# Convolution output weights cast by halves ahead of the norm, and later transposes behind the attention, in a two-layer fp32 decoder trunk

## The chip, the cores and the metric

The kernel runs on one core of one Trainium2 chip. The metric is the device time of one execution in microseconds (us); before the change the median of three runs is 2128.0 us (2128.0 to 2129.94).

## The reference, cut to what matters

There is one sequence of T = 1024 tokens with D = 1024 features. Layer 0 mixes tokens with a causal conformer convolution, layer 1 with sliding-window attention. Each layer adds the mixer's result to the stream and normalises, does the same around a squared-ReLU MLP, and adds a gated embedding.

```python
def conformer_conv(x, w_in, b_in, w_dw, b_dw, ln_g, ln_b, w_out, b_out):
    h = x @ w_in + b_in
    a, gate = jnp.split(h, 2, axis=-1)
    h = a * jax.nn.sigmoid(gate)
    h = lax.conv_general_dilated(h, w_dw[:, None, :], ...) + b_dw
    h = jax.nn.silu(layer_norm(h, ln_g, ln_b))
    return h @ w_out + b_out

def reference(x, p, ...):
    for i in range(DEPTH):                       # DEPTH = 2
        y = conformer_conv(...) if i < 1 else swa_sink_attention(...)
        x = layer_norm(DEEPNORM_ALPHA * x + y, mix_ln_g[i], mix_ln_b[i])
        x = layer_norm(DEEPNORM_ALPHA * x + sq_relu_mlp(x, ...), mlp_ln_g[i], mlp_ln_b[i])
        x = x + (p[i] @ ple_w_proj[i]) * jax.nn.sigmoid(x @ ple_w_gate[i])
    return x
```

## The kernel before

Every fp32 product is three matmuls on split operands. `split` casts a source to a high part (`wh` for weights, `xTh` for the transposed stream) on ScalarE, and VectorE subtracts to get the low part (`wl`, `xTl`); `mm3` then issues high by high, high by low and low by high. The stream is held as 8 tiles of 128 tokens, each in two halves of 512 features, and, transposed, as `xTh` and `xTl` in 8 blocks `kb` of 128 features.

Weights come as units of 128 x 1024, which are two blocks `kb` of 512 output columns. `prep` (L542) loads a unit into one of two `raw` buffers, casts it (L558) and subtracts (L559) into one of five `wh` and `wl` buffers. A `raw` buffer takes its next load only when both instructions of the unit before last have read it. The convolution's output projection `w_out` has eight units, here called U0 to U7: U0 to U3 hold the first 512 output columns, U4 to U7 the others. `mix_out` (L1048) makes them, and it alone gives `prep` a `gate`, an instruction that the load may not be ordered before. `tok_group` then holds four output banks in PSUM (names `ps`), one for each of four token tiles, and goes through the units.

The end of the convolution's norm is a chain over four engines: VectorE and GpSimd scale rows of tiles `X` and `A` by `sm`; TensorE transposes four 128 x 128 blocks into a bank; ScalarE applies SiLU from the bank (`z<-tr,cst` or `z<-ps,cst`); then `xTh` and `xTl` follow. Three banks rotate for the transposes, so every transpose waits for the `z` three before it. In this time ScalarE also copies the last tiles of the embedding product (`t<-ps`), which SyncE stores to `proj`. SyncE then loads eight pieces `E<-in_x_dram` of the stream.

In layer 1 the attention's output projection is finished by `out_tiles`, which calls `layer_norm` (L631) for each token tile. That normalises the tile in place on VectorE (tiles `A` and `B`) and calls `to_xT` (L603), which transposes both halves (`transpose4`) and splits them.

Nothing is issued as it is written. `Recorder.record` collects all instructions. `Recorder.schedule` walks them greedily with estimated costs and picks, on each engine, the ready one with the lowest place `prio`, which is the place of recording plus an offset that `later` sets. `slack` is added to the planned readiness of a marked instruction, so the plan treats its data as that much later; it adds no wait on the chip. The order on each engine is then fixed, and the chip keeps the order and waits by semaphores. Since `issue` emits every instruction from one line, all rows of the profile have the line L480.

Of the kernel before, what the change touches and what calls it, by code (L numbers as in the profile page):

```python
# [10 lines left out]
F32 = mybir.dt.float32  # L11
F32R = mybir.dt.float32r
AF = mybir.ActivationFunctionType
ALU = mybir.AluOpType
# [7 lines left out]
HT = 512  # L22
# [60 lines left out]
        2: [("weight",)], 3: [("out", 0)], 5: [("out", 1)],  # L83
    },
)
CST = 256 + 2 * NH
LANDING = dict(scr=4000.0, qd=5000.0, kd=5000.0, ad=5500.0, zd=6500.0, wsum=5000.0, proj=4500.0, xsp=4000.0, hid=4500.0)
SLACK = 900.0
# [424 lines left out]
class Emit:  # L513
# [28 lines left out]
    def prep(self, ap, blocks=None, gate=None):  # L542

        nc = self.nc
        raw = nc.tile("raw", (P, 1024), F32)
        wh = nc.tile("wh", (P, 1024), F32R)
        wl = nc.tile("wl", (P, 1024), F32R)
        if blocks:
            for j, kb in enumerate(blocks):
                cs = slice(j * 256, (j + 1) * 256)  # L550

                nc.sync.dma_start(raw[:, cs], ap[:, cs])
                self.split(raw[:, cs], wh[:, cs], wl[:, cs])
                self.load_xT(0, kb, nc.sync if kb else nc.scalar)
            return wh, wl
        with nc.after(gate) if gate else contextlib.nullcontext():
            nc.sync.dma_start(raw, ap)
        nc.scalar.copy(wh, raw)  # L558
        nc.vector.tensor_tensor(out=wl, in0=raw, in1=wh.bitcast(F32), op=ALU.subtract)  # L559
        return wh, wl  # L560

    def split(self, src, h, l):
# [37 lines left out]
    def blocks(self, a):  # L600
        return [a[:, j * P : (j + 1) * P] for j in range(4)]

    def to_xT(self, xt, t):  # L603

        for q in range(2):
            pv = self.transpose4(self.blocks(xt[q]), SLACK).rearrange("p (a b) -> p a b", a=4)
            sl = (slice(None), slice(4 * q, 4 * q + 4), slice(t * P, (t + 1) * P))
            self.split(pv, self.xTh[sl], self.xTl[sl])

# [22 lines left out]
    def layer_norm(self, t, gb, spill=None):  # L632

        nc = self.nc
        xt = self.x[t]
        mean, scale = self.stats(xt)
        for q in range(2):
            nc.vector.scalar_tensor_tensor(out=xt[q], in0=xt[q], scalar=mean, in1=gb[0][q], op0=ALU.subtract, op1=ALU.mult)
        for q in range(2):
            nc.vector.scalar_tensor_tensor(out=xt[q], in0=xt[q], scalar=scale, in1=gb[1][q], op0=ALU.mult, op1=ALU.add)  # L640
        self.to_xT(xt, t)
        if spill:
            for q in range(2):
                v = self.sb(("X", "zz")[q])
                nc.scalar.mul(v, xt[q], ALPHA)
                nc.sync.dma_start(spill[t][:, q * HT : (q + 1) * HT], v)
# [21 lines left out]
    def setup(self):  # L668
        nc, d = self.nc, self.d
        self.cc = self.const("cst", (P, CST), F32)[:, 0 : 32 + 64 + CG]  # L670
        self.ident = self.const("ident", (P, P), F32)
# [940 lines left out]
    def attention(self):  # L1612
        nc, d, ws = self.nc, self.d, self.ws
        ac = self.sb("cst", n=CST)
        nc.sync.dma_start(ac[:, 0:256], d["aconst"])
# [343 lines left out]
```

## Time and profile before

| | before |
|---|---|
| median of three runs | 2128.0 us |
| the profiled execution | 2127.52 us |
| its span, first to last instruction | 2125.8 us |
| TensorE (PE) busy | 2115.8 us |
| VectorE (DVE) busy | 1560.1 us |
| ScalarE (ACT) busy | 1046.2 us |
| GpSimd (POOL) busy | 201.1 us |

1.7 us lie around the span of the profiled execution. In timelines the columns are the start of a row, its length, engine, line, operation, output and inputs by their names without numbers, shape, and the count of instructions joined in the row; a bracket tells the idle time before it and what released it. PE and DVE records overlap a little, so the price of an instruction is read from one start to the next.

### The profile page before, as it was taken

Reading aid. Unit: us, or ns where it says so; the run is one execution under the profiler, and the core shown is the slowest. Engines: PE = TensorE matmul, PEld = TensorE weight load, DVE = VectorE, ACT = ScalarE, POOL = GpSimd, SP = SyncE. Lnnn points to the kernel's source line nnn. Section 1 sums busy time; section 2 is a strip of 40 time slices with the busy share of each in tenths; the row PEclk is TensorE's granted clock in tenths of the full one; section 3 lists DMA queues with packets and bytes.
Section 4 is the critical chain, followed back from the end, with each engine's and each line's share of the span. In section 5 each row is a group of like instructions: output and inputs, shape, how many; then the busy total and the mean of one; then the engine's idle time right before and its main releaser. Section 6 shows DMA issues by size and latency. Waiting matters only on the chain.

```text
span 2125.8 us, 28547 instructions
## 1 busy us (share of the span) xinstructions
PE 2115.8 (100%) x10067; PEld 1762.0 (83%) x10067; DVE 1560.1 (73%) x2359; ACT 1046.2 (49%) x1888; POOL 201.1 (9%) x391
## 2 busy tenths in 40 slices
PE   9999999999999999999999999999999999999999
PEld 7888888888888888888889888888888888888887
DVE  8766868966566787889554798796755658878993
ACT  7555743555555433341333797365555563333321
POOL 0000141000000200000000566100000011000010
PEclk9999999999999999999999999999999999999999
DMA  7679882347457955540567672364654598445223
GB/s 249 195 204 278 279 216 99 105 163 258 168 179 277 257 184 172 179 129 25 167 194 224 213 239 63 111 197 146 223 187 136 182 339 238 149 160 189 88 70 104
DMA packets 208078, 384.61 MB, mean 181 GB/s; under 512 B 28736, under 2 KB 82496, under 8 KB 207936
## 3 DMA queue, kind: packets, MB, share of 16 engines
q1 hardware_dynamic: 200880, 369.96, 53.0%
q0 software_dynamic: 6912, 12.59, 3.3%
q8 instruction: 79, 1.29, 0.2%
q14 instruction: 63, 0.52, 0.1%
q10 hardware_dynamic: 144, 0.26, 0.0%
HBM read 263.98 MB, written 114.56 MB: 178 GB/s over the span
## 4 chain that ended last, share of the span: by engine, by line
PE 95%; DVE 2%; DMA 2%; ACT 1%; issue 0%; POOL 0%; SPq 0%; DVEq 0%; ACTq 0%; POOLq 0%
PE ps L480 73%; PE tr L480 22%; DMA raw<-in_w_up_dram 1%; DVE A L480 1%; DVE wl L480 0%; DMA wh<-hid 0%; ACT z L480 0%; DVE sm L480 0%; DMA X<-in_xT_dram 0%; ACT t L480 0%; DVE t L480 0%; ACT wh L480 0%; DVE xTl L480 0%; POOL sm L480 0%; SPq L480 0%
## 5 line engine op out<-in xcount | busy, mean ns | idle before, releaser
L480 DVE TENSOR_TENSOR wl<-raw,wh 128x1024 fp32r<-128x1024 f32 (+2 forms) x144 | 151.6, 1053 | 141.4 <-ACT wh L480 141.1
L480 PE MATMUL ps<-xTl,xTh 128*128 128x512 f32 x628 | 244.3, 389 | 0.0
L480 PE MATMUL ps<-xTh,xTl 128*128 128x512 f32 x628 | 244.3, 389 | 0.0
L480 PE MATMUL ps<-xTh 128*128 128x512 f32 x628 | 244.1, 389 | 0.0
L480 PE MATMUL ps<-xTh,wh 128*128 128x512 f32 x608 | 238.7, 393 | 0.4 <-ACT xTh L480 0.3
L480 PE MATMUL ps<-xTl,wh 128*128 128x512 f32 x608 | 238.6, 392 | 0.1
L480 PE MATMUL ps<-xTh,wl 128*128 128x512 f32 x608 | 237.8, 391 | 0.0
L480 ACT CAST wh<-raw 128x1024 fp32r<-128x1024 f32 (+2 forms) x144 | 131.4, 913 | 200.8 <-PE ps L480 98.4
L480 PE MATMUL ps<-wl,xTh 128*128 128x512 f32 (+1 forms) x424 | 162.3, 383 | 0.0
L480 PE MATMUL ps<-wh,xTh 128*128 128x512 f32 (+1 forms) x424 | 161.5, 384 | 0.0
L480 PE MATMUL ps<-wh,xTl 128*128 128x512 f32 (+1 forms) x424 | 160.8, 380 | 0.4 <-DVE xTl L480 0.4
L480 DVE TENSOR_TENSOR wl<-g,wh 128x512 fp32r<-128x512 f32 x140 | 92.5, 686 | 90.0 <-ACT wh L480 90.0
L480 ACT CAST wh<-g 128x512 fp32r<-128x512 f32 x140 | 82.7, 621 | 150.1 <-PE ps L480 98.3
L480 ACT CAST xTh<-wh 128x1024 fp32r<-128x1024 f32 x78 | 81.9, 1050 | 123.2 <-PE ps L480 101.5
L480 PEld LDWEIGHTS ps<-xTl,xTh 128*128 128x128 f32 x628 | 117.9, 188 | 24.6
L480 PEld LDWEIGHTS ps<-xTh,xTl 128*128 128x128 f32 x628 | 117.9, 188 | 24.4
L480 PEld LDWEIGHTS ps<-xTh 128*128 128x128 f32 x628 | 117.9, 188 | 24.3
L480 PEld LDWEIGHTS ps<-xTh,wh 128*128 128x128 f32 x608 | 114.3, 188 | 25.8 <-ACT xTh L480 1.0
L480 PEld LDWEIGHTS ps<-xTh,wl 128*128 128x128 f32 x608 | 114.2, 188 | 23.4
L480 PEld LDWEIGHTS ps<-xTl,wh 128*128 128x128 f32 x608 | 114.3, 188 | 22.2 <-DVE xTl L480 0.8
L480 DVE TENSOR_TENSOR xTl<-wh,xTh 128x1024 fp32r<-128x1024 f32 x78 | 95.1, 1220 | 32.9 <-ACT xTh L480 32.8
L480 DVE TENSOR_TENSOR xTl<-wl,xTh 128x1024 fp32r<-128x1024 f32 x80 | 97.3, 1218 | 3.4 <-ACT xTh L480 3.4
(318 smaller groups left out, 4952.6 us busy)
## 6 DMA issues: line engine op xcount, KB each, us to landing
wh<-hid SPq DMA_DIRECT2D x80, 512.0 KB, 4.5
raw<-in_w_up_dram SPq DMA_DIRECT2D x64, 512.0 KB, 3.8
wl<-in_w_down_dram SPq DMA_DIRECT2D x60, 512.0 KB, 4.6
hid<-t SPq DMA_DIRECT2D x95, 256.0 KB, 2.4
hid<-zz SPq DMA_DIRECT2D x68, 256.0 KB, 3.5
raw<-hid SPq DMA_DIRECT2D x30, 512.0 KB, 4.3
z<-scr SPq DMA_DIRECT2D x32, 256.0 KB, 3.9
proj<-t SPq DMA_DIRECT2D x32, 256.0 KB, 3.8
```

The costliest lines, as they stand in the source:

```text
L480: getattr(getattr(nc, o.eng), o.name)(*a, **k)
```

## The change

Two things change. `prep` casts gated units, which are the eight of `w_out`, in two halves of 512 columns, and records cast and subtraction 100 places sooner. The load itself keeps its place and gate. `to_xT` takes its slack as an argument, and the norm behind the attention (the one that spills to `self.mid[1]`) gives 1700 where it gave 900; all other norms keep 900.

```diff
+HALVES = slice(0, HT), slice(HT, 2 * HT)
+SEAM = 1700.0
+SOONER = 100
 ...
 def prep(self, ap, blocks=None, gate=None):
         with nc.after(gate) if gate else contextlib.nullcontext():
             nc.sync.dma_start(raw, ap)
-        nc.scalar.copy(wh, raw)
-        nc.vector.tensor_tensor(out=wl, in0=raw, in1=wh.bitcast(F32), op=ALU.subtract)
+        with nc.later(-SOONER if gate else 0):
+            for c in HALVES if gate else (slice(0, 2 * HT),):
+                self.split(raw[:, c], wh[:, c], wl[:, c])
         return wh, wl
 ...
-    def to_xT(self, xt, t):
+    def to_xT(self, xt, t, slack):
         for q in range(2):
-            pv = self.transpose4(self.blocks(xt[q]), SLACK).rearrange("p (a b) -> p a b", a=4)
+            pv = self.transpose4(self.blocks(xt[q]), slack).rearrange("p (a b) -> p a b", a=4)
 ...
 def layer_norm(self, t, gb, spill=None):
-        self.to_xT(xt, t)
+        self.to_xT(xt, t, SEAM if spill is self.mid[1] else SLACK)
```

The order changes on ScalarE at the end of the convolution's norm. Before, the row of whole casts ahead of the first `z` holds U0 (`raw_617`) and U1 (`raw_630`), and U2 (`raw_742`) is cast behind the three copies `t`.

```order
L480 ACTIVATE X_600_2393<-X_600_2393,sm_61_125 128x512
L480 ACTIVATE A_592_2366<-A_592_2366,sm_61_125 128x512
L480 CAST wh_628_2519<-raw_617_2478 128x1024
L480 CAST wh_706_2962<-raw_630_2524 128x1024
L480 ACTIVATE z_688_2860<-tr_713_3014,cst_337 128x512
```

```order
L480 CAST xTh_340<-z_755_3212 128x512
L480 COPY t_718_3049<-ps_717_3040 128x512
L480 ACTIVATE z_760_3238<-tr_758_3222,cst_337 128x512
L480 COPY t_721_3062<-ps_719_3055 128x512
L480 CAST xTh_340<-z_760_3238 128x512
L480 COPY t_723_3073<-ps_720_3058 128x512
L480 CAST wh_739_3154<-raw_742_3171 128x1024
```

Now the same two stretches read as follows.

```order
L483 ACTIVATE X_600_2393<-X_600_2393,sm_61_125 128x512
L483 ACTIVATE A_592_2366<-A_592_2366,sm_61_125 128x512
L483 CAST wh_628_2519<-raw_617_2478 128x512 x2
L483 CAST wh_706_2962<-raw_630_2524 128x512
L483 ACTIVATE z_688_2860<-tr_713_3014,cst_337 128x512
```

```order
L483 CAST xTh_340<-z_754_3211 128x512
L483 CAST wh_706_2962<-raw_630_2524 128x512
L483 COPY t_718_3049<-ps_717_3040 128x512
L483 CAST wh_739_3154<-raw_742_3176 128x512
L483 ACTIVATE z_764_3256<-tr_757_3223,cst_337 128x512
L483 CAST wh_739_3154<-raw_742_3176 128x512
L483 CAST xTh_340<-z_764_3256 128x512
L483 ACTIVATE z_767_3274<-ps_758_3236,cst_337 128x512
L483 COPY t_721_3062<-ps_719_3055 128x512
L483 COPY t_723_3073<-ps_720_3058 128x512
```

Three halves instead of two whole casts stand ahead of the first `z`; U1's second half and both halves of U2 stand ahead of the last two copies `t`, and one `z` has passed the copies.

On SyncE's queue, at the loads for `w_out`, two units (U2 and U3) stood ahead of the `proj` stores before.

```order
L480 DMA raw_742_3171<-in_w_out_dram 128x1024
L480 DMA raw_749_3188<-in_w_out_dram 128x1024
L480 DMA proj_5_88_152<-t_718_3049 128x512
L480 DMA proj_6_89_153<-t_721_3062 128x512
L480 DMA proj_7_90_154<-t_723_3073 128x512
L480 DMA E_702_2946<-in_x_dram 128x512 x2
L480 DMA E_710_2983<-in_x_dram 128x512 x2
L480 DMA E_712_3009<-in_x_dram 128x512 x2
L480 DMA E_714_3027<-in_x_dram 128x512 x2
```

Now U3 (`raw_790`) stands behind the stores and the eight loads of the stream.

```order
L483 DMA raw_742_3176<-in_w_out_dram 128x1024
L483 DMA proj_5_88_152<-t_718_3049 128x512
L483 DMA proj_6_89_153<-t_721_3062 128x512
L483 DMA proj_7_90_154<-t_723_3073 128x512
L483 DMA E_702_2946<-in_x_dram 128x512 x2
L483 DMA E_710_2983<-in_x_dram 128x512 x2
L483 DMA E_712_3009<-in_x_dram 128x512 x2
L483 DMA E_714_3027<-in_x_dram 128x512 x2
L483 DMA raw_790_3378<-in_w_out_dram 128x1024
L483 DMA raw_801_3415<-in_w_out_dram 128x1024
```

U3's load has moved behind eleven transfers, and U4's (`raw_801`) follows it directly; the other rows kept their places.

On TensorE, behind the attention, the last token tiles have four transposes of tiles `A` (the rows with `ident`), here called T1 to T4. Before, they stood so among the matmuls of the next product:

```order
L480 MATMUL ps_2330_13119<-ident_338,A_2245_12629 128x128 x4
L480 MATMUL ps_2346_13194<-wh_2318_13063,wh_2328_13109 128x512
L480 MATMUL ps_2340_13167<-ident_338,A_2250_12657 128x128 x4
L480 MATMUL ps_2346_13194<-wl_2317_13061,wh_2328_13109 128x512
L480 MATMUL ps_2346_13194<-wh_2318_13063,wl_2326_13104 128x512
```

```order
L480 MATMUL ps_2347_13198<-wl_2317_13061,wh_2328_13109 128x512
L480 MATMUL ps_2343_13174<-ident_338,A_2252_12665 128x128 x4
L480 MATMUL ps_2347_13198<-wh_2318_13063,wl_2326_13104 128x512
L480 MATMUL tr_2352_13217<-wh_2318_13063,wh_2269_12742 128x512
L480 MATMUL tr_2352_13217<-wl_2317_13061,wh_2269_12742 128x512
L480 MATMUL tr_2352_13217<-wh_2318_13063,wl_2268_12740 128x512
L480 MATMUL tr_2352_13217<-wh_2318_13063,wh_2328_13109 128x512
L480 MATMUL tr_2352_13217<-wl_2317_13061,wh_2328_13109 128x512
L480 MATMUL ps_2369_13281<-ident_338,A_2253_12667 128x128 x4
L480 MATMUL tr_2352_13217<-wh_2318_13063,wl_2326_13104 128x512
```

Now the last two and their neighbours read:

```order
L483 MATMUL tr_2352_13233<-wh_2318_13079,wh_2269_12758 128x512
L483 MATMUL tr_2352_13233<-wl_2317_13077,wh_2269_12758 128x512
L483 MATMUL tr_2352_13233<-wh_2318_13079,wl_2268_12756 128x512
L483 MATMUL ps_2343_13190<-ident_338,A_2252_12681 128x128 x4
L483 MATMUL ps_2373_13307<-ident_338,A_2253_12683 128x128 x4
L483 MATMUL tr_2352_13233<-wh_2318_13079,wh_2325_13109 128x512
L483 MATMUL tr_2352_13233<-wl_2317_13077,wh_2325_13109 128x512
```

T1 and T2 stand three matmuls later, T3 four; T4 stands two matmuls sooner, directly behind T3.

## The prediction

> **What bounds the kernel now.** The head of the page comes first: the span, the busy time of the engines and the chain of work that ended last.
>
> ```profile
> span 2125.8 us, 28547 instructions
> PE 2115.8 (100%) x10067; PEld 1762.0 (83%) x10067; DVE 1560.1 (73%) x2359; ACT 1046.2 (49%) x1888; POOL 201.1 (9%) x391
> PE 95%; DVE 2%; DMA 2%; ACT 1%; issue 0%; POOL 0%; SPq 0%; DVEq 0%; ACTq 0%; POOLq 0%
> ```
>
> TensorE is the bound: 2125.8 - 2115.8 = 10 us of the span are not its work. The change neither adds nor removes TensorE work, so it can gain only from that rest. The table of waits says which part.
>
> ```profile
> PE ps L480 <- DVE t L480: 1.5, 1, 1.5
> PE ps L480 <- ACT t L480: 1.2, 2, 0.7
> PE ps L480 <- DVE A L480: 0.7, 2, 0.5
> PE tr L480 <- ACT z L480: 0.7, 1, 0.7
> PE ps L480 <- DVE xTl L480: 0.4, 1, 0.4
> ```
>
> The change's two places own three rows: `z` and `xTl` at the end of the convolution's norm (0.7 + 0.4 us) and `A` behind the attention (0.7 us in two waits). If all went and nothing came, that would be 1.8 us, 0.09%. About 0.2% (4.3 us) is what a measurement of this kernel can tell from no change, so a measurable gain is as good as excluded. The question is what new wait could arise.
>
> The TensorE timeline at the first place:
>
> ```profile
> 264.47 0.40 PE L480 MATMUL ps<-wh,wl 128*128 128x512 f32 x1
> 265.60 0.66 PE L480 MATMUL tr<-ident,X 128*128 128x128 f32 x4 [0.73 <-ACT z L480]
> ...
> 268.35 0.50 PE L480 MATMUL ps<-wh,xTl 128*128 128x512 f32 x1 [0.37 <-DVE xTl L480]
> ...
> 283.46 1.30 PE L480 MATMUL ps<-wh,xTh 128*128 128x512 f32 x5
> 284.60 0.39 PE L480 MATMUL ps<-wl,xTh 128*128 128x512 f32 x1
> ```
>
> After the two stalls TensorE runs without a gap; five matmuls take 284.60 - 283.46 = 1.14 us, so one takes 0.228.
>
> **Part 1: what the halves save.** ScalarE and VectorE there:
>
> ```profile
> 262.89 1.98 ACT L480 CAST wh<-raw 128x1024 fp32r<-128x1024 f32 x2
> 264.77 0.77 ACT L480 ACTIVATE z<-tr,cst 128x512 f32<-128x512 f32 x1
> 265.44 0.76 ACT L480 ACTIVATE z<-ps,cst 128x512 f32<-128x512 f32 x1
> ...
> 268.47 0.63 ACT L480 CAST xTh<-z 128x512 fp32r<-128x512 f32 x1
> 268.98 0.79 ACT L480 ACTIVATE z<-ps,cst 128x512 f32<-128x512 f32 x1
> ...
> 272.97 0.63 ACT L480 COPY t<-ps 128x512 f32<-128x512 f32 x1
> 273.45 1.11 ACT L480 CAST wh<-raw 128x1024 fp32r<-128x1024 f32 x1
> 274.40 0.83 ACT L480 ACTIVATE z<-ps,cst 128x512 f32<-128x512 f32 x1
> ```
>
> ```profile
> 265.28 1.21 DVE L480 TENSOR_TENSOR wl<-raw,wh 128x1024 fp32r<-128x1024 f32 x1
> 266.41 1.29 DVE L480 TENSOR_SCALAR X<-X,sm 128x512 f32<-128x512 f32 x2
> 267.62 0.67 DVE L480 TENSOR_TENSOR xTl<-z,xTh 128x512 fp32r<-128x512 f32 x1
> ```
>
> From start to start, a whole cast takes 274.40 - 273.45 = 0.95 us, a 512-column cast 268.98 - 268.47 = 0.51, a `z` 265.44 - 264.77 = 0.67, a copy `t` 273.45 - 272.97 = 0.48; on VectorE a whole `wl` 266.41 - 265.28 = 1.13, one 512-column step (267.62 - 266.41) / 2 = 0.605, which I take for half a `wl`. Three half casts instead of two whole ones ahead of the first `z`: 3 x 0.51 - 2 x 0.95 = -0.37 us, so the first stall shrinks by 0.37. Three half subtractions instead of two whole ones: 3 x 0.605 - 2 x 1.13 = -0.44, so `X` and the first `xTl` come 0.44 earlier. TensorE passes both stalls about **0.44 us earlier**; at most the whole 0.73 + 0.37 = 1.10 goes.
>
> Splitting costs 2 x 0.51 - 0.95 = 0.07 us on ScalarE and 2 x 0.605 - 1.13 = 0.08 on VectorE per unit. [...]
>
> **Part 2: what the halves delay.** SyncE's queue:
>
> ```profile
> 265.31 1.54 SPq L480 DMA_DIRECT2D raw<-in_w_out_dram  x2
> 271.47 2.48 SPq L480 DMA_DIRECT2D proj<-t  x3
> 274.04 4.91 SPq L480 DMA_DIRECT2D E<-in_x_dram  x8
> ...
> 284.46 2.67 SPq L480 DMA_DIRECT2D raw<-in_w_out_dram  x2
> ```
>
> Before, U2 and U3 were issued at 265.3. Now U3's `raw` buffer comes free only after U1's second half is cast and subtracted, and its load stands behind three `proj` stores and eight loads of `E`. When do these end? The stores wait for the last copy `t`. ScalarE has no slack that could absorb extra work ahead of it:
>
> ```profile
> 263.00:284.00 21.00, 19.89 (x117) 16.15 (x116) 17.55 (x29) 20.88 (x32) 15.71 (x12) 1.00 0.74 226
> ```
>
> (busy columns are PE, PE load, DVE, ACT, POOL: ACT 20.88 of 21.00.) Ahead of that copy now stand six half casts for two whole ones and one `z` more: 6 x 0.51 - 2 x 0.95 + 0.67 = 1.83 us. So it starts at 274.80, the `E` loads are issued from 275.9 to 280.8 instead of 274.04 to 278.95, and U3's load goes out at about 280.8.
>
> When does it land? The issue table for one late `E` load (issued at 278.5) and one `raw` load (issued at 284.5), each with KB and us to landing, and the window between:
>
> ```profile
> E<-in_x_dram SPq DMA_DIRECT2D x1, 256.0 KB, 9.8
> ```
>
> ```profile
> raw<-in_w_out_dram SPq DMA_DIRECT2D x1, 512.0 KB, 6.9
> ```
>
> ```profile
> 280.00:284.00 4.00, 4.00 (x23) 3.33 (x22) 3.87 (x7) 3.88 (x7) 0.88 (x1) 1.00 1.10 268
> ```
>
> The DMA engines are full (share 1.10, 268 GB/s), so a load lands when what is queued ahead has drained. Before, the late `E` load landed at 278.5 + 9.8 = 288.3; now that is between 288.3 (the queue drains as before) and 290.15 (1.83 later), middle 289.2. U3's 512 KB behind it take 1.95 us at 268 GB/s, or twice that if GpSimd's loads of `B` get half; middle 2.9. Landing: about **292.1**, outer ends 287.7 (280.8 + 6.9) and 294.0.
>
> When is it wanted? Behind the place at 283.46, now 283.02, TensorE has 33 matmuls to U3's first one (24 of U2, 9 of other units): 283.02 + 33 x 0.228 = 290.5. The first half cast adds 0.51 and about 0.1 of signalling: 292.1 + 0.6 - 290.5 = **2.2 us of new stall**; from 287.7 it would be none, from 294.0 it would be 4.1. The matching subtraction (0.605) is covered by the three `wh` matmuls of other banks that now stand first (0.68). U4, directly behind U3, is wanted only after 24 matmuls of U3 and another group; but VectorE must subtract U4 before it empties the first output bank, which may cost up to 0.2 more. Later loads have room. I put nothing for these.
>
> **Part 3: transposes behind the attention.** At the last tiles TensorE and VectorE do this:
>
> ```profile
> 1396.46 0.63 PE L480 MATMUL ps<-ident,A 128*128 128x128 f32 x4 [0.25 <-DVE A L480]
> ...
> 1399.89 0.63 PE L480 MATMUL ps<-ident,A 128*128 128x128 f32 x4 [0.50 <-DVE A L480]
> ...
> 1401.75 0.62 PE L480 MATMUL ps<-ident,A 128*128 128x128 f32 x4
> ```
>
> ```profile
> 1399.66 1.28 DVE L480 TENSOR_TENSOR xTl<-ps,xTh 128x512 fp32r<-128x512 f32 x2
> 1400.86 0.74 DVE L480 SCALAR_TENSOR_TENSOR A<-A,sm,g 128x512 f32<-128x512 f32 x1
> ```
>
> T1, three matmuls later, loses its wait of 0.25, T3, four later (0.9 us), its 0.50. But T4 now follows T3 directly. Its tile needs the step that was at 1400.86, which VectorE now does ahead of the two `xTl`, and its bank is T1's, free only after T1's `xTl`. That comes at about 1399.66 + 0.74 + 0.605 = 1401.0, so T4 starts near 1401.1. Without stalls TensorE would be there at 1401.75 - 0.75 - 2 x 0.228 = 1400.5, so T4 waits about 0.55. Gain: 0.75 - 0.55 = **0.2 us**, between 0 and 0.75. The earlier tiles of this norm are reordered in the same way; none of their transposes has a row among the waits, and later places leave their data more time, so I put nothing for them.
>
> **Sum.** -0.44 + 2.2 - 0.2 = +1.6 us on the profiled execution: 2127.5 + 1.6 = 2129.1 (span 2125.8 + 1.6 = 2127.4; 1.7 around it). The median of before lies 0.5 above that execution, so I forecast a median of **2129.6 us**.
>
> **The rivals.**
>
> *U3 lands in time* (0.25). Speaking for it: 6.9 us to landing for a `raw` load behind the same kind of traffic gives 287.7. Against: a 256 KB load issued earlier took 9.8. Then only gains are left: 2128.0 - 0.44 - 0.2 = 2127.4, at the outside 2126.2 with all 1.8 us.
>
> *U3 lands very late and TensorE falls back to its starting speed* (0.11, the slower side). The first matmuls of the trace:
>
> ```profile
> 1.51 3.35 PE L480 MATMUL ps<-t 128*128 128x512 f32 x7 [1.51 <-DVE t L480]
> ```
>
> Seven take 3.35 us, 0.48 each instead of 0.228. If the stall is long enough to bring that back, a first stretch of 3.35 us loses 3.35 - 7 x 0.228 = 1.75. With U3 at the late end and 0.2 for the output bank: 4.1 + 1.75 + 0.2 - 0.64 = +5.4, hence 2133.4. The total passes 4.3 us when the stall passes 4.3 + 0.64 - 1.75 - 0.2 = 3.0, that is when U3 lands after 292.9. Against it: later waits in this trace are 0.7 us at most, so nothing shows that a stall of 3 brings the slow start back; and the granted clock (the column ahead of the DMA share) reads 1.00 in that stretch too, so it may have another cause:
>
> ```profile
> 1.50:5.00 3.50, 3.35 (x7) 2.15 (x7) 0.38 (x1) 1.83 (x3) 0.00 (x0) 1.00 0.85 250
> ```
>
> [...]
>
> *The head does not gain and the tail does not stall* (0.09). Only U1's first half is ahead of the norm, its `wl` second half comes 12 us later, and T4 pays back T3: 2128.0. For it: every term here is under 2.5 us; against: the second stall's releaser is plainly the subtraction that has been cut.
>
> The forecast has 0.55. Its own ends are 2128.0 - 0.64 = 2127.4 with no stall and 2128.0 + 4.1 + 0.2 - 0.64 = 2131.7 without the clock. The range goes from 2126.5, for the case of gains, to 2132.5; most of the slow case lies beyond. Slower by over 0.2% means over 2132.3: 0.11, the second rival. Faster by over 0.2% needs 4.3 us where 1.8 are to be had: 0.03. The rest, 0.86, is within.
>
> **What would show it.** The span of the profiled execution near 2127.4. At 265.2 the first transposes start with a wait of about 0.35 for `z`, and the wait for `xTl` is no longer than before. SyncE issues one `raw` at 265.3 and the next at about 280.8, landing at 291 to 293, and TensorE waits about 2.2 us near 290.5 for `wh` out of that `raw`. Near 1400 the wait for `A` is under 0.3 and one near 1401 for T1's `xTl` is new. I am wrong if TensorE has no wait near 290.5 (then the queue drains faster than I take it), if it waits over 3 us there or its matmuls behind it are 0.4 us apart, or if a wait arises between 266 and 283 since ScalarE now hands out `z` and `xTh` up to 0.68 us later around 272.

## The result, and the profile after

The changed kernel takes 2134.09 us, the median of seven runs (2131.11 to 2135.52), against 2128.0 us before. The ratio is 1.0029, with a 95% interval of 1.0017 to 1.0040: **slower by 0.29%**, some 6.1 us, where the forecast was +1.6 us and a range up to 2132.5. The profiled execution has a span of 2132.2 us. The head of the page and the head of TensorE's table of waits:

```profile
span 2132.2 us, 28560 instructions
PE 2119.0 (99%) x10067; PEld 1764.5 (83%) x10067; DVE 1560.2 (73%) x2367; ACT 1046.3 (49%) x1896; POOL 201.7 (9%) x391
```

```profile
PE ps L483 <- ACT wh L483: 4.4, 1, 4.4
...
PE tr L483 <- ACT z L483: 0.4, 1, 0.4
...
PE ps L483 <- DVE xTl L483: 0.3, 1, 0.3
```

One wait of 4.4 us is new, and TensorE is busy 3.2 us longer with the same instructions. The waits for `z` and `xTl` have shrunk, and the waits for `A` are gone. The timeline of TensorE at the new wait:

```profile
290.25 0.39 PE L483 MATMUL ps<-wh,xTl 128*128 128x512 f32 x1
295.02 1.65 PE L483 MATMUL ps<-wh,xTh 128*128 128x512 f32 x3 [4.39 <-ACT wh L483]
296.47 0.63 PE L483 MATMUL ps<-wl,xTh 128*128 128x512 f32 x1
296.89 0.63 PE L483 MATMUL ps<-wh,xTl 128*128 128x512 f32 x1
...
300.16 0.39 PE L483 MATMUL ps<-wh,xTl 128*128 128x512 f32 x1
300.39 0.39 PE L483 MATMUL ps<-wl,xTh 128*128 128x512 f32 x1
```

The matmul at 295.02 is U3's first. From 290.25 to 295.02 is 4.77 us instead of 0.23: 4.5 us lost. Behind it matmuls start 296.89 - 296.47 = 0.42 us apart, from 300.16 on 0.23 again. The 12 matmuls from 295.02 to 300.16 take 5.14 us instead of 12 x 0.228 = 2.74, so the slow stretch costs a further 2.4 us. ScalarE and the issue table (KB, us to landing) show what it waited for:

```profile
294.35 1.14 ACT L483 CAST wh<-raw 128x512 fp32r<-128x512 f32 x2 [11.12 <-DMA raw<-in_w_out_dram]
```

```profile
raw<-in_w_out_dram SPq DMA_DIRECT2D x1, 512.0 KB, 9.0
```

SyncE's queue, and GpSimd's steps after and before:

```profile
265.32 0.33 SPq L483 DMA_DIRECT2D raw<-in_w_out_dram  x1
271.58 4.58 SPq L483 DMA_DIRECT2D proj<-t  x3
276.26 9.01 SPq L483 DMA_DIRECT2D E<-in_x_dram  x8
285.36 2.75 SPq L483 DMA_DIRECT2D raw<-in_w_out_dram  x2
```

```profile
268.85 4.91 POOL L483 TENSOR_SCALAR A<-A,sm 128x512 f32<-128x512 f32 x4
273.71 2.94 POOL L483 DMA_DIRECT2D B<-bo  x3
```

```profile
269.36 5.86 POOL L480 TENSOR_SCALAR A<-A,sm 128x512 f32<-128x512 f32 x4
275.17 3.09 POOL L480 DMA_DIRECT2D B<-bo  x3
```

U3 is issued behind the `E` loads, as forecast, but at 285.4 and not at 280.8: the eight `E` loads take 9.01 us to issue where they took 4.91. GpSimd's loads of the bias (`B<-bo`) start 1.46 us sooner than before, and `E` 2.2 us later, so GpSimd's queue is now ahead of `E` where it was behind.

Behind the attention, T1 to T4:

```profile
1404.48 0.60 PE L483 MATMUL ps<-ident,A 128*128 128x128 f32 x4
...
1405.15 0.60 PE L483 MATMUL ps<-ident,A 128*128 128x128 f32 x4
...
1407.44 1.03 PE L483 MATMUL ps<-ident,A 128*128 128x128 f32 x8
```

None of them has a wait; T3 and T4 are one row of eight.

### The profile page after: what moved, and what is told of

Same layout as the page of the kernel before. It is cut to its first block, busy times and chain, and to the rows that moved or that the text cites. A ratio compares the mean times of both kernels' runs of the same rounds, so it can differ in the third digit from the quotient of the medians.

```text
span 2132.2 us, 28560 instructions
## 1 busy us (share of the span) xinstructions
PE 2119.0 (99%) x10067; PEld 1764.5 (83%) x10067; DVE 1560.2 (73%) x2367; ACT 1046.3 (49%) x1896; POOL 201.7 (9%) x391
## 4 chain that ended last, share of the span: by engine, by line
PE 96%; DMA 2%; DVE 1%; ACT 1%; issue 0%; SPq 0%; POOL 0%; DVEq 0%; ACTq 0%
PE ps L483 73%; PE tr L483 22%; DMA raw<-in_w_out_dram 0%; DMA wh<-hid 0%; DMA raw<-in_w_up_dram 0%; ACT z L483 0%; DMA hid<-z 0%; DVE A L483 0%; DVE sm L483 0%; DVE t L483 0%; DVE wl L483 0%; SPq L483 0%; ACT wh L483 0%; ACT t L483 0%; DMA raw<-in_w_in_dram 0%
```

## The experiments

All were run beside the kernel before on the same chip, and times are medians with the ratio to before and its 95% interval. The theory (A): the split frees U3's `raw` buffer late, the load falls behind `E` and its traffic, and TensorE's long idle time also costs it the clock. The rivals: the halves themselves, the order behind the attention, or another cause of the slow matmuls.

**One part alone.** `seam_only` casts whole units at the old place:

```diff
-        with nc.later(-SOONER if gate else 0):
-            for c in HALVES if gate else (slice(0, 2 * HT),):
+        with nc.later(0):
+            for c in (slice(0, 2 * HT),):
```

> Only the later transposes behind the attention; the convolution's weights are cast whole, as before. Theory A (the whole loss comes from U3's late load): no wait for wh, clock 1.00 throughout, and both waits for A near 1396 and 1400 gone, so 0.7 to 1.1 us faster than before: about 2127.0 us. Rival C (the new order behind the attention costs part of the loss): at least 1 us slower than before, 2129 or more.

Measured: 2125.39 against 2125.53 us, 0.9996 (0.9987 to 1.0005). `halves_only` is the other part:

```diff
-SEAM = 1700.0
+SEAM = 900.0
```

> Only the halves of w_out, recorded 100 places sooner; the transposes keep the slack of 900. Theory A: the wait of 4 us for U3's wh near 290 and the half-speed matmuls behind it stay, and the two waits for A (0.7 us) come back: about 2135 us, 7 above before. Rival C: 2130 or less, since the loss would leave with the transposes.

Measured: 2132.30 us, 1.0029 (1.0018 to 1.0040), with this wait:

```profile
PE ps L483 <- ACT wh L483: 4.5, 1, 4.5
```

The whole loss comes with the halves. The two waits for `A` were expected back in `halves_only` and did not come: with its transposes at the old places it has no wait for `A`, and neither has `seam_only` with the later ones. So these two traces do not show what the later places do (more on that below), and their effect on the time can't be told from nothing.

**Without halves, still sooner.**

```diff
-            for c in HALVES if gate else (slice(0, 2 * HT),):
+            for c in (slice(0, 2 * HT),):
```

> The changed kernel with whole casts instead of halves, still 100 places sooner. U3's load is back at its old place on SyncE's queue, since U1 is cast whole ahead of the first z; E starts later by about two whole casts and one z (2.5 us), U4 and U5 stand behind E. Theory A (the split frees the buffer late, not the sooner casting): no wait for U3, head stalls of 0.7 and 0.4 us as before, 0.5 to 1.3 us below before from the transposes; if U4 is late as it was with U3 ahead of E, VectorE is held by U4's subtraction and a wait of 1 to 3 us for an output bank appears near 296.

Measured: 2129.13 against 2126.43 us, 1.0011 (1.0002 to 1.0020). U3 is back at its old place and isn't waited for, but U4, behind `E`, is late. VectorE must subtract it before it empties an output bank:

```profile
298.48 0.68 PE L483 MATMUL ps<-wh,xTh 128*128 128x512 f32 x1 [2.38 <-DVE B L483]
```

So the sooner casting does harm of its own: it delays the copies `t`, and with them `proj`, `E` and the load behind. Here too GpSimd's loads start first (274.72 against 276.59), and the `E` loads take 9.96 us to issue. Matmuls 0.43 us apart follow this wait as well.

**U3 ahead of `E`.** Two kernels. `late_E` leaves ScalarE's order alone and moves the `E` loads behind U5:

```diff
-                with nc.after((last, done[0])[t // 4]):
+                with nc.after((last, done[1])[t // 4]):
```

> The changed kernel with the eight loads E of the stream placed behind U3, U4 and U5 on SyncE's queue; ScalarE's order is unchanged. Theory A: U3 is issued at about 280, as soon as its buffer is free, lands by 285, TensorE doesn't wait for it, the clock stays at 1.00: about 2126.7 us, 1.3 below before, if the later E loads delay nothing. Rival B (the halves themselves cost: more instructions on ScalarE and z and xTh later around 272): the time stays at 2132 or more.

Measured: 2124.81 against 2125.53 us, 0.9996 (0.9988 to 1.0005). U3 is issued at 279.5, its cast starts at 285.1, and nothing waits for it:

```profile
285.06 1.14 ACT L483 CAST wh<-raw 128x512 fp32r<-128x512 f32 x2 [2.03 <-DMA raw<-in_w_out_dram]
```

All halves and all their extra instructions are still there, so these cost nothing that can be measured. `u3_before_E` gets there by casting sooner:

```diff
-SOONER = 100
+SOONER = 150
```

> The changed kernel with 150 places instead of 100: U1's second half is cast right behind its first z's, U3's load stands ahead of the E loads on SyncE's queue. Theory A: U3 is issued by 277 and lands by 282, no wait for it, clock 1.00, about 1 us below before. If U4's load, now behind E, is the next to be late, a wait of 1 to 3 us for its wh appears 5 us later and the time is 0 to 3 us above before.

Measured: 2131.72 against 2126.00 us, 1.0028 (1.0018 to 1.0037). U3 lands by 282.6, but now U4 stands behind `E`, and VectorE is held by it:

```profile
298.93 0.50 PE L483 MATMUL ps<-wh,xTh 128*128 128x512 f32 x1 [2.66 <-DVE B L483]
```

The stall was sized rightly, but half-speed matmuls (0.42 to 0.43 us apart from 299.96 to 302.94, granted clock 0.50 from 300 to 301) follow it here too, which the expectation for this case left out. `sooner_300` brings U3 to its old place and U4 and U5 ahead of `E`:

```diff
-SOONER = 100
+SOONER = 300
```

> The changed kernel with 300 places instead of 100: halves, U3 at its old place on SyncE's queue, U4 and U5 ahead of the E loads. Theory A: no wait for any wh of w_out and none for an output bank over 0.3 us, head stalls 0.4 and 0.3 us, clock 1.00: 0.5 to 1.5 us below before. Against it: E is issued later still, up to 279, and may be late for the second group of tiles; then a wait for E or its bias appears near 310.

Measured: 2125.87 against 2126.43 us, 0.9996 (0.9987 to 1.0005), with no wait for weights or output banks. The first stall is worse than expected (0.9 us for `z`, 0.5 for `xTl`), since another order stands at the head.

**Why `E` is issued so slowly.** `thin_bias` makes GpSimd's loads tiny, so it leaves out most of the bias:

```diff
-                    nc.gpsimd.dma_start(xt[q], bo[q], accum_op=ALU.add)
+                    nc.gpsimd.dma_start(xt[q][:, 0:8], bo[q][:, 0:8], accum_op=ALU.add)
```

> The changed kernel with GpSimd's 16 loads that add the output bias cut to 8 of 512 columns, so most of the bias is left out; all other instructions keep their order. Theory A1 (U3 is late because the E loads, issued 2 us later than before, now share the DMA engines with GpSimd's loads): the E loads are issued in 5 us instead of 9, U3 at about 281 and lands at 286 to 289, no wait over 0.3 us: about 2126.7 us. Theory A2 (the queue's order alone makes it late): U3 lands after 292 still, wait over 2 us, 2131 or more.

Measured: 2125.35 against 2125.53 us, 0.9996 (0.9987 to 1.0005); `E` is issued in 4.10 us, U3 at 280.2. That removes bytes as well as their start, so `bias_late` keeps every byte and only delays GpSimd, by four multiplications by 1:

```diff
+        for v in bo + bo:
+            with nc.after(done[1]):
+                nc.gpsimd.tensor_scalar(out=v, in0=v, scalar1=1.0, scalar2=0.0, op0=ALU.mult, op1=ALU.add)
+            nc.ops[-1].dur = 0.0
 ...
-SOONER = 100
+SOONER = 104
```

(The 104 makes up for the four places that they take in the recording.)

> The changed kernel with four multiplications by 1 on GpSimd ahead of its bias loads, so that these start about 4 us later, behind the first loads E as they did before the change; no byte is left out, other orders are the same. Theory A1a (the E loads are slow since GpSimd's loads, which now start first, take half the DMA engines): E is issued in 5 to 6 us instead of 9, U3 at 281 to 282.5, lands at 288 to 291, wait 0 to 1.5 us, clock 1.00, 0 to 1.5 us below to 1 above before. Theory A1b (the amount alone matters, not which queue starts): U3 still lands after 293, 5 us or more above before.

Measured: 2128.13 against 2126.00 us, 1.0009 (1.0000 to 1.0017).

```profile
276.24 4.86 SPq L483 DMA_DIRECT2D E<-in_x_dram  x8
281.19 2.10 SPq L483 DMA_DIRECT2D raw<-in_w_out_dram  x2
```

```profile
277.46 2.86 POOL L483 DMA_DIRECT2D B<-bo  x3
```

```profile
raw<-in_w_out_dram SPq DMA_DIRECT2D x1, 512.0 KB, 10.6
```

```profile
292.48 0.96 PE L483 MATMUL ps<-wh,xTh 128*128 128x512 f32 x3 [1.47 <-ACT wh L483]
```

With GpSimd's loads behind the first `E` again, `E` is issued in 4.86 us and U3 at 281.2. It lands at 281.2 + 10.6 = 291.8, TensorE waits 1.47 us and keeps its clock (1.00 from 290 to 298). The same bytes, started in another order, make 4 us of difference for the load behind. U3 lands 0.8 us behind its expected range, and the time is 1.1 us above the expected end. The profiled execution, at 2126.99 us, is one of the faster ones, so its trace does not show where the rest of the median goes.

**What makes the matmuls slow.** 18 matmuls more, into a bank that nothing reads, right ahead of U3's first one:

```diff
 ...
+                for k in range(18):
+                    self.nc.tensor.matmul(dm, self.xs(0, 0, P)[0], us[2][0][:, 0:HT], start=True, stop=True)
 ...
```

> The changed kernel with 18 matmuls more, right ahead of U3's first one, into a bank that nothing reads; all other orders are the same. They fill 18 x 0.228 = 4.1 us of the 4.4 us wait. Theory A (the loss is 4.5 us of stall plus 2.4 us of half-speed matmuls that the idle time causes): the clock stays at 1.00, U3's first matmul still starts near 295, the matmuls behind it are 0.228 us apart, and the time is 1.6 to 2.4 us below the changed kernel, 4 to 5 us above before. Rival D (the slow matmuls come from something else at that place, such as the arriving loads): they stay 0.43 apart and the time is that of the changed kernel or more, 6 to 7 us above before.

Measured: 2131.42 against 2126.00 us, 1.0024 (1.0014 to 1.0034), with the clock at 1.00. Since this was judged against another set of runs of the changed kernel, both were run side by side:

> The changed kernel once more, on the chip of the next run, for comparison with it: 6 to 7 us above before, a wait of 4 to 4.6 us for U3's wh and 8 to 12 half-speed matmuls behind it.

> The changed kernel with 18 matmuls more, into a bank that nothing reads, in the wait for U3, on the same chip as the changed kernel itself. Theory A (idle time causes the half clock): full clock behind the wait, 1.6 to 2.4 us below the changed kernel on this chip. Rival D (something else causes it): no difference or slower.

Measured: 2132.49 us (1.0028, 1.0018 to 1.0037) for the changed kernel and 2130.90 us (1.0020, 1.0011 to 1.0029) with the filling, before 2126.43. The windows (the last columns are granted clock, DMA share, GB/s) behind the wait, first of the changed kernel and then with the filling:

```profile
294.00:298.00 4.00, 2.98 (x7) 2.40 (x8) 2.26 (x4) 2.28 (x4) 1.32 (x2) 0.50 1.11 259
298.00:302.00 4.00, 4.00 (x14) 3.13 (x14) 3.09 (x6) 0.00 (x0) 2.14 (x3) 0.76 1.09 300
```

```profile
294.00:298.00 4.00, 3.04 (x14) 2.08 (x13) 1.29 (x2) 1.78 (x4) 1.72 (x2) 1.00 1.13 250
298.00:302.00 4.00, 4.00 (x20) 3.30 (x19) 3.92 (x7) 0.50 (x1) 1.75 (x2) 1.00 1.15 271
```

The loads still arrive in these windows, but the clock stays up: the idle time causes the half clock. In the medians the filling gains 1.6 us, the low end of what was expected; the two intervals overlap, so the gain in time rests on the trace more than on the medians. With 8 matmuls, to see whether the idle time that is left is enough (the edit against `fill18`):

```diff
-                for k in range(18):
+                for k in range(8):
```

> As with 18, but 8 matmuls: 1.8 us of the wait filled, 2.6 us of idle time left. In the changed kernel the clock fell 2.5 us after TensorE's last matmul and came back 6.8 us later, with halves alone 5.1 us after it and back 3.4 us later. [...]

Measured: 2131.53 against 2126.00 us, 1.0028 (1.0018 to 1.0039), 5.5 us above before, where `fill18` stood 5.4 above the same runs, so the times do not tell the two apart. The traces do: here TensorE waited 2.46 us and the clock fell (0.50 from 297 to 298):

```profile
294.75 1.28 PE L487 MATMUL ps<-wh,xTh 128*128 128x512 f32 x3 [2.46 <-ACT wh L487]
```

No version is shown to be faster than before: `late_E`, `seam_only` and `sooner_300` all stand at 0.9996 with 1 inside the interval.

## Why the prediction was wrong

The sign, the place and the chain were right: U3's load goes behind `proj` and `E`, and TensorE waits for its `wh` near 290. The time that came is nearer to the second rival (2133.4, given 0.11) than to the forecast.

- **The step that failed** is "the `E` loads are issued from 275.9 to 280.8". Their start was right (276.26), and their length was taken from before (4.91 us) and came out at 9.01. The prediction moved `E` and did not ask what else was queued there: GpSimd's loads of the bias started at 275.17 before, 1.13 us behind the first `E`, so an `E` from 275.9 on already stands behind them. They started sooner still (273.71), since GpSimd's steps ran faster (four `A` in 4.91 us for 5.86). Where `E` started 1.13 and 1.22 us ahead of GpSimd's loads (before and `bias_late`), it took 4.91 and 4.86 us to issue; where it started 2.55 and 1.87 us behind them (the changed kernel and `whole_sooner`), 9.01 and 9.96. (In the other runs with whole bias loads it took 5.58 in `seam_only`, 5.63 in `sooner_300` and 5.88 in `late_E`, and 8.75 to 9.46 elsewhere.) The DMA engines were full meanwhile (share 1.07 from 276 to 284); that the loads of one queue hold up those of the other there is my estimate from that share, and no run shows how the order acts. `bias_late` shows the size of it: with that order restored U3 is issued at 281.2 and lands at 291.8, against 280.8 and 292.1 in the prediction, and the wait is 1.47 us against 2.2. Why GpSimd's steps ran faster wasn't tried; VectorE has less to do beside them (5.63 us busy from 266 to 274, before 6.93), which may be the reason:

```profile
266.00:274.00 8.00, 7.62 (x46) 5.98 (x45) 6.93 (x12) 8.00 (x15) 8.00 (x6) 1.00 0.51 176
```

```profile
266.00:274.00 8.00, 7.74 (x45) 6.18 (x46) 5.63 (x10) 8.00 (x15) 8.00 (x7) 1.00 0.32 101
```

- **The outer end was too near.** I gave 294.0 as the latest landing; it was 285.4 + 9.0 = 294.4, a wait of 4.39 us against at most 4.1. (The 290.15 on the way to it is 288.3 + 1.83 = 290.13, which changes nothing.) The steps around it held: TensorE got to U3 at 290.48 (forecast 290.5), and the cast at 294.35 freed its matmul 0.67 us later (forecast 0.6).
- **The clock was named, but priced too low and held for too unlikely.** The second rival gave one slow stretch of 3.35 us, 1.75 us lost; the stretch lasted 4.9 us (295.02 to 299.95), and about 2.4 were lost. I took a stall of 3 us as unproven and gave it 0.11, though the row of slow first matmuls was there. What I held against it, a granted clock of 1.00 at those first matmuls, is no reading: the trace before has its first record of the clock at 5.55 us, and the view prints 1.00 where there is no record. The slow matmuls end close behind that first record: they are 0.23 us apart from 6.23 us on in this trace, and from 6.44 in the changed kernel's, whose first record is at 6.40. `fill8` shows that 2.46 us can be enough, `whole_sooner` that 2.38 can.
- **The head** came as worked out: the wait for `z` fell from 0.73 to 0.40 us, that for `xTl` from 0.37 to 0.26, together 0.44.
- **Behind the attention** all 0.75 us of waits went, where 0.2 was forecast, but the later places are not shown to have done it. The waits hang on a weight load. On VectorE the subtraction `wl` of a `w_up` unit stands ahead of the steps on `A`, and before it was held until that unit was loaded and cast:

```profile
1393.10 1.23 DVE L480 TENSOR_TENSOR wl<-raw,wh 128x1024 fp32r<-128x1024 f32 x1 [1.36 <-ACT wh L480]
```

In `halves_only` it was held for 0.48 us only, and T1 and T3, at their old places, have no wait:

```profile
1397.90 1.23 DVE L483 TENSOR_TENSOR wl<-raw,wh 128x1024 fp32r<-128x1024 f32 x1 [0.48 <-ACT wh L483]
```

```profile
1401.73 0.60 PE L483 MATMUL ps<-ident,A 128*128 128x128 f32 x4
...
1404.68 0.63 PE L483 MATMUL ps<-ident,A 128*128 128x128 f32 x4
```

In the changed kernel's execution it was not held at all. VectorE's two subtractions start at 1406.66 there, so T1's bank is free at 1406.66 + 0.605 = 1407.27, ahead of T4 at about 1407.8:

```profile
1406.66 1.28 DVE L483 TENSOR_TENSOR xTl<-ps,xTh 128x512 fp32r<-128x512 f32 x2
```

`late_E` is the run that tests the forecast, with the later places and VectorE held as long as before. It has no wait for `A`, and T4 waits 0.54 us for `xTl`, where 0.55 was forecast:

```profile
1392.25 1.23 DVE L483 TENSOR_TENSOR wl<-raw,wh 128x1024 fp32r<-128x1024 f32 x1 [1.30 <-ACT wh L483]
```

```profile
1400.20 0.66 PE L483 MATMUL ps<-ident,A 128*128 128x128 f32 x4 [0.54 <-DVE xTl L483]
```

So this term was right for the conditions that it was worked out from. That the `w_up` unit comes sooner in some executions was not foreseen, and why it does wasn't tried.
- **The cost of splitting** was rightly put near nothing: `late_E` holds every extra cast and isn't slower. The delay through the copies was the real price.

For the convolution the profiled executions give 4.5 + 2.4 - 0.44 = 6.5 us, which is the whole of the 6.4 us of span. Matched one by one, TensorE's matmuls are as early as before at 264 us, 6.5 us later than before at 300, 7.7 at 1390, 6.6 at 1410 and 6.4 at the end. So what is gained behind the attention had been lost between 400 and 700 us in that same execution, over small waits far from the change.

## What to carry to other kernels

When an edit delays one engine's work, list every load whose buffer or whose place in a queue hangs on that work, and ask of each load in flight beside it whether it still starts in the same order: a queue that isn't touched can come to stand ahead of one that is. A consumer that has been fed early enough by far may have only one buffer of lead; splitting its last read, which looks free, moves the next load by all that is queued in between. The engine that a wait names may itself be waiting: ask what held it before you price the wait's end. Here TensorE waits of 2.38 us and more cost the clock and those of 1.47 us and less did not, so a long wait is priced with a second term for the clock.

## What the runs showed of the hardware

How soon the clock fell, and for how long, did not go with the length of the wait. In the changed kernel the granted clock (third column from the end) falls at about 293.1 and comes back at about 299.95:

```profile
292.50:293.00 0.50, 0.00 (x0) 0.00 (x0) 0.00 (x0) 0.00 (x0) 0.08 (x1) 1.00 1.05 291
293.00:293.50 0.50, 0.00 (x0) 0.00 (x0) 0.00 (x0) 0.00 (x0) 0.00 (x0) 0.62 1.11 303
...
299.50:300.00 0.50, 0.50 (x3) 0.40 (x2) 0.47 (x2) 0.00 (x0) 0.40 (x1) 0.55 1.05 418
300.00:300.50 0.50, 0.50 (x4) 0.41 (x3) 0.26 (x1) 0.00 (x0) 0.00 (x0) 1.00 1.04 377
```

That is 6.8 us. Four traces with a fall, in us from the span's start (the wait is a length):

| run | TensorE's wait | its last matmul ends | it starts again | clock falls | clock is back |
|---|---|---|---|---|---|
| changed kernel | 4.39 | 290.6 | 295.02 | 293.1 | 299.95 |
| `halves_only` | 4.51 | 290.9 | 295.37 | 295.96 | 299.4 |
| `fill8` | 2.46 | 292.3 | 294.75 | 295.2 | 298.6 |
| `u3_before_E` | 2.66 | 296.3 | 298.93 | 299.96 | 303.4 |

The clock fell 2.5 to 5.1 us behind the last matmul, in three of the four only when TensorE was at work again, and stayed down for 3.4 us in these three and 6.8 us in the changed kernel. In `bias_late`, with its wait of 1.47 us, it reads 1.00 in every window from 286 to 308. What sets these two times was not shown.

The slow first matmuls did not end at the same time in every execution: the first record of the clock is at 5.55 us in the trace before and at 6.40 in the changed kernel's, where the first matmul starts at 1.51 and 1.52 us.

How fast one queue's loads were issued went with what another queue had in flight. Eight loads `E` went out in 4.10 us while GpSimd's loads were tiny (`thin_bias`), in 4.91 and 4.86 us when these started 1.13 and 1.22 us behind them (before, `bias_late`), and in 9.01 and 9.96 us when these had started 2.55 and 1.87 us before them (the changed kernel, `whole_sooner`). `bias_late` and the changed kernel load the same bytes.
